# Later places for four steps of the delta heads, and the state's two products side by side

## The chip, the cores and the metric

One core of a Trainium2 chip runs the kernel. The metric is the device time of one execution in microseconds (us), as the median of several runs. Engines are named as in the profile: PE is TensorE (matmuls), DVE VectorE, ACT ScalarE, POOL GpSimd, SP SyncE, which here only issues transfers.

## What is computed

One layer of an encoder, for a prompt of 512 rows and a later chunk of 64 rows that share all weights. The input projection is split into a gated delta rule with 4 heads, a differential attention with 4 heads and a pooling mixer; their outputs are joined, projected back, and a convolutional feed-forward block follows. The change lies in the delta heads:

```python
kk = jnp.einsum('bhncd,bhnsd->bhncs', k, k)
lmat = jnp.where(strict, beta[..., :, None] * decay * kk, 0.0)
uw = lax.linalg.triangular_solve(eye + lmat, rhs, left_side=True, lower=True, unit_diagonal=True)
...
def step(state, xs):
    u_c, w_c, qg_c, qk_c, kt_c, gl_c = xs
    delta = u_c - jnp.einsum('bhcd,bhde->bhce', w_c, state)
    o = jnp.einsum('bhcd,bhde->bhce', qg_c, state) + jnp.einsum('bhcs,bhse->bhce', qk_c, delta)
    state = state * gl_c[..., None, None] + jnp.einsum('bhcd,bhce->bhde', kt_c, delta)
    return state, o
```

The output of each head is then normalised and multiplied by a gate, SiLU(z).

## The kernel before

**The stream.** Most of PE's time goes to gemms: the 576 rows (512 + 64) are the columns of the moving operand, in pieces of 256 and 320, and each weight tile of 128 x 1024 is split into two numbers, `w_hi` (a cast on ACT, L174) and `w_lo` (a subtraction on DVE, L175). A gemm of the input projection is 48 matmuls into a bank `g`. A gemm's end is followed on ACT or DVE by an instruction that empties its bank: L578 for the rows that go through the short convolution, L924 for the attention's rows.

**The planner.** The delta heads and the attention are generators. They `yield` a number, and a clock that adds the nominal time of every matmul issued decides when a generator goes on; its products go into other banks, `m` (four of them), between two matmuls of the stream. `spawn(gen, delay)` starts one. A stream that has to wait for a flag lets the clock jump to the next generator that is due. So the numbers after `yield` fix how many `g` matmuls stand on PE between two steps. PE keeps the order in which the program issues. The other engines' instructions are ordered by a scheduler, and each engine runs its own row in that order.

**The delta heads.** `front(h)` (L609) transposes the keys, the queries and the values of a head (L89 by way of `tokens`), squares them on ACT (L628, L632), scales keys and values (ACT L646) into `kt` and `vs`, and forms five products kk, one for each of five chunks `c` (four of 128 rows, one of 64). The rows to be transposed come from the convolution: DVE taps (L596) and a last product (L601). `levels` (L705) inverts the triangular matrices of two heads in steps of doubling size; its last two steps make `X64` (copied by ACT, L754) and the corner of `XT`. `scan(c)` (L763) goes through the chunks in the order 4, 0, 1, 2, 3, all four heads at once: the state `S` times the key rows gives `R` (DVE), the inverse times `R` gives `e` (copied by ACT, L791), the state times the query rows follows, then `kt` times `e` (the new state, DVE L803) and a product with `e` for the output. Chunk 0 begins without a state. `delta_out` (L825) scales a head's output rows (DVE L833, five instructions), lets 2500 of the clock pass, transposes them, and multiplies them with the gate (L840, L841); `hi` (ACT L844) and `lo` (DVE L845) of the result go to the output projection.

**What waits for what at the end.** When all four heads are through `delta_out`, the attention starts; `value_rows` of its head 0 transposes the values, which sets the flag `values0`. The stream's `attn_proj(3)` waits for that flag before its last projection (L918), since the tile for the values is free only then. The first scores (`ckT` and `kq`) come after that.

Of the kernel before, what the change touches and what calls it, by code (L numbers as in the profile page):

```python
# [11 lines left out]
AF = mybir.ActivationFunctionType  # L12
ALU = mybir.AluOpType
# [46 lines left out]
def hybrid_step(ctx: ExitStack, tc: tile.TileContext, I, O):  # L60
# [30 lines left out]
    def spawn(gen, delay=0):  # L91
        active.append([clock[0] + delay, gen])
# [456 lines left out]
    with ExitStack() as ctx2:  # L549
# [59 lines left out]
        def front(h):  # L609
# [37 lines left out]
            U = dq.tile([P, 5, 2, P], F32, name="U", bufs=4)  # L647
            nc.gpsimd.memset(U[:, 4, :, NS:], 0.0)
            for c in range(5):
                yield 600  # L650
                n = P if c < 4 else NS
                r = slice(starts[c], starts[c] + n)
                kk = bank()[:, :2 * n].rearrange("p (i t) -> p i t", i=2)
                mm(kk, kT[:, starts[c]:starts[c] + P], kq[h][:, :, r])
                Dm = dq.tile([P, P], F32, name="tq", bufs=2)[:, :n]
                nc.vector.scalar_tensor_tensor(Dm, sums[:, c, :n], gsum[:, c, h:h + 1], mneg[:, :n],
                                               op0=ALU.subtract, op1=ALU.add)
                nc.scalar.activation(Dm, Dm, AF.Exp)
                nc.vector.scalar_tensor_tensor(U[:, c, :, :n], kk, w[:, c:c + 1],
                                               Dm.unsqueeze(1).broadcast_to([P, 2, n]), op0=ALU.mult, op1=ALU.mult)  # L660
# [44 lines left out]
        def levels(pair, inv):  # L705
# [44 lines left out]
            for f in pair:  # L750
# [1 line left out]
                for c in range(4):  # L752
                    mm(pa[64:, c * 64:c * 64 + 64], f["K"][:64, c, 64:], f["X64"][:64, c])
                nc.scalar.copy(f["X64"][64:], pa[64:, :256].rearrange("p (c x) -> p c x", c=4))  # L754
            yield 1200
            for f in pair:
                XT = f["T"]
                pa = bank()
# [4 lines left out]
        def scan(c):  # L763
# [14 lines left out]
            for f in heads:  # L778
                f["pa"] = bank()
                if f["S"] is None:  # L780
                    f["R"] = f["vs"][:, c]
                else:
                    mm(f["pa"][:n, 0:P], kq[f["h"]][:, 0, starts[c]:starts[c] + n], f["S"])
                    f["R"] = dq.tile([P, P], F32, name="R", bufs=4)
                    nc.vector.scalar_tensor_tensor(f["R"][:n], f["pa"][:n, 0:P], ngam[:n, c, f["h"]:f["h"] + 1],
                                                   f["vs"][:n, c], op0=ALU.mult, op1=ALU.add)
            yield 1000
            for f in heads:
                mm(f["pa"][:n, P:2 * P], f["T"][:n, c, :n], f["R"][:n])
                f["e"] = dq.tile([P, P], F32, name="e", bufs=4)  # L790
                nc.scalar.copy(f["e"][:n], f["pa"][:n, P:2 * P])  # L791
            if heads[0]["S"] is not None:
                for f in heads:
                    mm(f["pa"][:n, 0:P], kq[f["h"]][:, 1, starts[c]:starts[c] + n], f["S"])
            else:
                yield 420
            for f in heads:
                mm(f["pa"][:, 2 * P:3 * P], f["kt"][:n, c], f["e"][:n])
                Sn = dq.tile([P, P], F32, name="S", bufs=8)
                if f["S"] is None:  # L800
                    nc.vector.tensor_copy(Sn, f["pa"][:, 2 * P:3 * P])
                else:
                    nc.vector.scalar_tensor_tensor(Sn, f["S"], last[:, c, f["h"]:f["h"] + 1],  # L803
                                                   f["pa"][:, 2 * P:3 * P], op0=ALU.mult, op1=ALU.add)
                f["Sn"] = Sn
            for f in heads:
                mm(f["pa"][:n, 3 * P:4 * P], f["Q"][:n, c, :n], f["e"][:n])
            for f in heads:
                oraw = f["o"]
                if f["S"] is None:  # L810
                    nc.scalar.copy(oraw[:n, c], f["pa"][:n, 3 * P:4 * P])
                else:
                    tq = dq.tile([P, P], F32, name="tq", bufs=2)
                    nc.scalar.activation(tq[:n], f["pa"][:n, 0:P], AF.Copy, scale=gam[:n, c, f["h"]:f["h"] + 1])
                    nc.vector.tensor_add(oraw[:n, c], tq[:n], f["pa"][:n, 3 * P:4 * P])
                tq = dq.tile([P, P], F32, name="tq", bufs=2)
                nc.scalar.activation(tq[:n], oraw[:n, c], AF.Square, accum_out=f["sso"][:n, c:c + 1])
                f["S"] = f["Sn"]
                if c == 4:
                    nc.sync.dma_start(O["s_delta"][f["h"]], f["S"])  # L820
                if c == 3:
                    nc.sync.dma_start(O["p_delta"][f["h"]], f["S"])
# [275 lines left out]
        def projections():  # L1098
            nonlocal dq
            for h in range(HEADS):  # L1100
                kq[h], vT[h] = kq_tile(), v_tile()
                first = first_products() if h == 0 else None
                for i, t in enumerate((4 + h, h, 8 + h)):
                    early_rows = h == 0 and i < 2
                    ps = next(first) if early_rows else (yield from gemm(hmix))
                    if not early_rows:
                        yield from after("scaled")
                    conv_rows(t, vT[h] if i == 2 else kq[h][:, i], ps, not early_rows)
                    if h == 0 and i == 1:
                        next(first, None)  # L1110
                        spawn(finish_start(), 3000)
                    if h == 1 and i == 0:
                        yield from after("start")
                        dq = dstack.enter_context(tc.tile_pool(name="delta", bufs=1, reuse_waits="tile"))
                        spawn(front(0), 3500)
                if h:
                    spawn(front(h), 6500)
            spawn(gates(), 0)
# [326 lines left out]
```

## Time and profile before

| what | us |
|---|---|
| median of 3 runs | 851.34 (850.49 to 851.52) |
| the profiled execution | 850.96 |
| its span, first to last instruction | 849.1 |
| outside the span | 1.9 |
| PE busy in the span | 829.5 (98%) |
| DVE, ACT, POOL busy | 536.0, 359.9, 109.5 |

The mean granted clock of TensorE is 0.999. Start times count from the span's beginning. A timeline's row joins instructions of one kind that follow each other, so its duration is that of all of them, and in brackets at its end stands the idle time before it with the instruction that ended it. The delta heads' work lies between about 45 and 275 us.

### The profile page before, as it was taken

The numbers are of one execution on the slowest core, as the hardware profiler recorded it, in microseconds if no ns is written. First come the engines' busy times: TensorE is split into PE (matmuls) and PEld (weight loads), VectorE is DVE, ScalarE is ACT, GpSimd is POOL, SyncE is SP. The second block draws the span as 40 slices with busy tenths as digits, with TensorE's granted clock in tenths as the row PEclk, the third lists the DMA queues.
The fourth block names the chain that finished last, engine by engine and source line by source line (L and its number), as shares of the span: only waits on it lengthen the run. The fifth ranks groups of instructions, "written<-read, shape, count | busy, mean of one in ns | idle before, by whom it ended". The sixth has DMA issues, their size and how long they took to land.

```text
span 849.1 us, 15939 instructions
## 1 busy us (share of the span) xinstructions
PE 829.5 (98%) x6342; PEld 803.9 (95%) x6342; DVE 536.0 (63%) x1203; ACT 359.9 (42%) x798; POOL 109.5 (13%) x166
## 2 busy tenths in 40 slices
PE   9989999999999999999999999999999999999996
PEld 8989999999999877789999999999999999999996
DVE  6798867881348667765767777776776773223423
ACT  7366661163444644543544444444434432222322
POOL 3132211220002000000011121121211210000001
PEclk9999999999999999999999999999999999999999
DMA  6242223242204323326622222222222223323313
GB/s 247 76 125 81 62 72 101 96 117 81 77 32 142 107 80 120 98 77 227 226 75 97 78 75 100 76 78 96 76 84 92 75 74 107 103 87 97 113 58 112
DMA packets 39032, 84.83 MB, mean 100 GB/s; under 512 B 9386, under 2 KB 14526, under 8 KB 38958
## 3 DMA queue, kind: packets, MB, share of 16 engines
q1 hardware_dynamic: 38014, 82.57, 30.1%
q10 hardware_dynamic: 944, 1.25, 0.4%
q8 instruction: 50, 0.82, 0.4%
q14 instruction: 24, 0.20, 0.1%
HBM read 72.98 MB, written 10.82 MB: 99 GB/s over the span
## 4 chain that ended last, share of the span: by engine, by line
PE 89%; DVE 4%; DMA 2%; ACT 2%; issue 1%; SPq 0%; POOLq 0%; POOL 0%; DVEq 0%; ACTq 0%
PE g L85 75%; PE m L85 11%; PE m L89 3%; DMA w_raw<-in_ffn_down_dram 1%; ACT w_hi L174 1%; DVE w_lo L175 1%; DMA x<-in_xT_dram 1%; DVE tmp L890 0%; DVE kq L596 0%; DMA w_raw<-in_w_out_dram 0%; ACT wide L348 0%; DVE oatt L1047 0%; DVE kq L601 0%; DVE p L1016 0%; DVE tmp L578 0%
## 5 line engine op out<-in xcount | busy, mean ns | idle before, releaser
L85 PE MATMUL g<-wide,w_hi 128*128 128x256 f32 x1472 | 265.6, 301 | 0.3
L85 PE MATMUL g<-t,w_hi 128*128 128x256 f32 (+1 forms) x1408 | 242.9, 294 | 0.0
L85 PEld LDWEIGHTS g<-wide,w_hi 128*128 128x128 f32 x1472 | 222.3, 190 | 2.9 <-DVE wide L349 0.6
L85 PEld LDWEIGHTS g<-t,w_hi 128*128 128x128 f32 x1408 | 210.2, 188 | 0.0
L174 ACT CAST w_hi<-w_raw 128x1024 fp32r<-128x1024 f32 (+2 forms) x109 | 110.9, 1017 | 172.8 <-PE g L85 161.8
L85 PE MATMUL g<-wide,w_lo 128*128 128x256 f32 x736 | 160.9, 300 | 0.5 <-DVE w_lo L175 0.5
L175 DVE TENSOR_TENSOR w_lo<-w_raw,w_hi 128x1024 fp32r<-128x1024 f32 (+2 forms) x109 | 128.2, 1176 | 49.9 <-ACT w_hi L174 48.9
L85 PE MATMUL g<-t,w_lo 128*128 128x256 f32 x704 | 150.2, 295 | 0.0
L85 PEld LDWEIGHTS g<-wide,w_lo 128*128 128x128 f32 x736 | 123.7, 190 | 2.5 <-issue 1.1
L85 PEld LDWEIGHTS g<-t,w_lo 128*128 128x128 f32 x704 | 117.4, 188 | 0.1
L1298 DVE SCALAR_TENSOR_TENSOR c<-u,par,c 128x511 f32<-128x511 f32 (+3 forms) x176 | 79.0, 512 | 2.5 <-ACT c L1294 2.5
L1301 POOL COPY fout<-u 128x4 f32<-128x4 f32 x44 | 51.2, 1163 | 223.1 <-DVE u L1292 223.1
L1292 DVE TENSOR_TENSOR u<-g,rstd 128x576 f32<-128x576 f32 x44 | 33.3, 758 | 59.7 <-PE g L85 58.2
L85 PE MATMUL g<-w,w_hi 128*128 128x256 f32 (+1 forms) x280 | 48.4, 295 | 0.0
L85 PEld LDWEIGHTS g<-w,w_hi 128*128 128x128 f32 x280 | 42.0, 188 | 0.0
L1294 ACT ACTIVATE c<-u,par 128x576 f32<-128x576 f32 x44 | 38.4, 873 | 4.6 <-DVE u L1292 1.8
L1318 ACT ACTIVATE s<-c 128x576 f32<-128x576 f32 x22 | 15.1, 688 | 45.8 <-DVE c L1300 45.8
L267 POOL TENSOR_TENSOR osc<-sso,mhalf 128x5 f32<-128x5 f32 x8 | 9.4, 1183 | 182.7 <-DVE sso L1042 77.9
L85 PE MATMUL g<-w,w_lo 128*128 128x256 f32 (+1 forms) x140 | 29.9, 294 | 0.0
L1203 ACT ACTIVATE junk<-m 128x128 f32<-128x128 f32 (+1 forms) x38 | 10.3, 274 | 40.2 <-PE m L89 32.2
L85 PE MATMUL g<-kq,w_hi 128*128 128x256 f32 (+1 forms) x128 | 25.0, 304 | 0.0
L1204 DVE TENSOR_TENSOR t<-m,nf 128x128 f32<-128x128 f32 (+1 forms) x38 | 10.6, 289 | 21.9 <-ACT junk L1203 21.9
(325 smaller groups left out, 1019.8 us busy)
## 6 DMA issues: line engine op xcount, KB each, us to landing
w_raw<-in_ffn_up_dram SPq DMA_DIRECT2D x44, 512.0 KB, 3.2
w_raw<-in_w_in_dram SPq DMA_DIRECT2D x30, 512.0 KB, 3.2
w_raw<-in_ffn_down_dram SPq DMA_DIRECT2D x16, 512.0 KB, 3.6
w_raw<-in_w_out_dram SPq DMA_DIRECT2D x8, 512.0 KB, 3.9
w_raw<-in_ffn_down_dram SPq DMA_DIRECT2D x8, 384.0 KB, 3.2
xr<-in_xT_dram SPq DMA_DIRECT2D x8, 288.0 KB, 3.2
x_d<-xr SPq DMA_DIRECT2D x8, 288.0 KB, 2.1
w<-x_d SPq DMA_DIRECT2D x8, 288.0 KB, 5.2
```

The costliest lines, as they stand in the source:

```text
L85: ordered(nc.tensor.matmul(out, lhsT=lhsT, rhs=rhs, start=start, stop=stop), n / 2.4 if rhs.dtype == F32R else max(54, n / 0.6))
L89: ordered(nc.tensor.transpose(out=out, in_=in_, identity=identity), 107)
L174: nc.scalar.copy(hi[:, :kt], raw)
L175: last_split[0] = nc.vector.tensor_sub(lo[:, :kt], raw, hi[:, :kt].bitcast(F32)).ins
L267: nc.gpsimd.tensor_tensor(out, x, epst[:x.shape[0], :x.shape[1]], op=ALU.pow)
L1203: nc.scalar.activation(junk[:n], src, AF.Square, scale=D ** -0.5, accum_out=op["part"][:n, c, m:m + 1])
L1204: nc.vector.tensor_mul(op["yt"][c][m // 4][:n, (m % 4) * P:(m % 4 + 1) * P], src, op["nf"][:n, m * P:(m + 1) * P])
L1292: nc.vector.tensor_mul(u, ps[:, O0:O1], rstd)
L1294: nc.scalar.activation(c, u, AF.Identity, scale=fw[:, 2, t:t + 1], bias=col("ffn_conv_b", t))
L1298: nc.vector.scalar_tensor_tensor(c[:, a + d:b], u[:, a:b - d], fw[:, j, t:t + 1], c[:, a + d:b], op0=ALU.mult, op1=ALU.add)
L1301: nc.gpsimd.tensor_copy(fout[:, :, :, t], u[:, NP - 64:].rearrange("p (s c) -> p s c", c=64)[:, :, 62:])
L1318: nc.scalar.activation(s, cv[0], AF.Silu)
```

## The change

Four numbers grow: head 0's front starts 7000 instead of 3500 of the clock after its cause, the first kk of every front waits 1700 instead of 600, the last step of `levels` waits 2100 instead of 1200, and in `scan` 900 pass between the copies `e` and the products that use them (before: none, or 420 in chunk 0). And in `scan` both products with the state, of the key rows and of the query rows, are issued at a step's beginning; two regions of the bank change places for that.

```diff
@@ front
             for c in range(5):
-                yield 600
+                yield 600 if c else 1700
@@ levels
-            yield 1200
+            yield 2100
             for f in pair:
                 XT = f["T"]
@@ scan
-                    mm(f["pa"][:n, 0:P], kq[f["h"]][:, 0, starts[c]:starts[c] + n], f["S"])
+                    for i in range(2):
+                        mm(f["pa"][:n, 2 * i * P:2 * i * P + P], kq[f["h"]][:, i, starts[c]:starts[c] + n], f["S"])
...
-            if heads[0]["S"] is not None:
-                for f in heads:
-                    mm(f["pa"][:n, 0:P], kq[f["h"]][:, 1, starts[c]:starts[c] + n], f["S"])
-            else:
-                yield 420
+            yield 900
             for f in heads:
-                mm(f["pa"][:, 2 * P:3 * P], f["kt"][:n, c], f["e"][:n])
+                mm(f["pa"][:, 0:P], f["kt"][:n, c], f["e"][:n])
...
-                    nc.scalar.activation(tq[:n], f["pa"][:n, 0:P], AF.Copy, scale=gam[:n, c, f["h"]:f["h"] + 1])
+                    nc.scalar.activation(tq[:n], f["pa"][:n, 2 * P:3 * P], AF.Copy, scale=gam[:n, c, f["h"]:f["h"] + 1])
@@ projections
-                        spawn(front(0), 3500)
+                        spawn(front(0), 7000)
```

Three places show what this does to the engines' rows. Line numbers after `scan` are smaller by 3 in the changed kernel.

DVE, around head 0's query rows. `kq_150` holds head 0's keys and queries, `kq_534` head 1's; `g_536` and `g_621` are the two gemms of head 1's. Before:

```order
L578 TENSOR_TENSOR tmp_604<-g_536,rstd1_126 128x512
...
L596 SCALAR_TENSOR_TENSOR kq_150<-tmp_304,ah_131,kq_150 128x579 x2
...
L596 SCALAR_TENSOR_TENSOR kq_534<-tmp_604,ah_131,kq_534 128x579
L484 TENSOR_REDUCE lam_138<-lprod_480 128x2
L491 TENSOR_SCALAR qneg_130<-qscale_129 128x5
L439 TENSOR_TENSOR fcor_132<-fcor_132,fcor_t_493 128x44
L601 SCALAR_TENSOR_TENSOR kq_150<-tmp_304,kq_150 128x579
...
L578 TENSOR_TENSOR tmp_713<-g_621,rstd1_126 128x512
```

and now:

```order
L596 SCALAR_TENSOR_TENSOR kq_150<-tmp_304,ah_131,kq_150 128x579
L578 TENSOR_TENSOR tmp_676<-g_621,rstd1_126 128x512
...
L596 SCALAR_TENSOR_TENSOR kq_150<-tmp_304,ah_131,kq_150 128x579
...
L596 SCALAR_TENSOR_TENSOR kq_534<-tmp_604,ah_131,kq_534 128x579
L175 TENSOR_TENSOR w_lo_692<-w_raw_626,w_hi_691 128x1024
L484 TENSOR_REDUCE lam_138<-lprod_480 128x2
L491 TENSOR_SCALAR qneg_130<-qscale_129 128x5
L596 SCALAR_TENSOR_TENSOR kq_534<-tmp_676,ah_131,kq_534 128x579
L439 TENSOR_TENSOR fcor_132<-fcor_132,fcor_t_493 128x44
L601 SCALAR_TENSOR_TENSOR kq_150<-tmp_304,kq_150 128x579
```

The evacuation of `g_621`, a tap on it and a `w_lo` have moved ahead of head 0's L601. On PE the transposes of head 0's keys stand 30 `g` later than before, 12 behind the last matmul of `g_621` (before: 30 into that gemm), and those of the queries 14 behind the keys' in both.

PE, a step of the scan with a state (`R` and `e` as above, `XT` the inverse). Before:

```order
L85 MATMUL m<-R,XT 128x128 x4
L85 MATMUL m<-S,kq 128x128 x4
L85 MATMUL m<-e,kt 128x128 x4
L85 MATMUL m<-e,U 128x128 x4
L85 MATMUL g<-wide,w_hi 128x256
```

and now, where the step begins with both products and 10 `g` stand between them and `R`'s, as before:

```order
L85 MATMUL m<-S,kq 128x128 x8
...
L85 MATMUL m<-R,XT 128x128 x4
L85 MATMUL g<-wide,w_hi 128x256
...
L85 MATMUL g<-wide,w_hi 128x320
L85 MATMUL m<-e,kt 128x128 x4
L85 MATMUL m<-e,U 128x128 x4
```

Eight `g` matmuls now follow `R`'s products. In `levels`, 18 instead of 10 stand between the last two steps.

PE, from head 0's output transposes (`U`) to the value rows (`vT`). Before, 22 `g` stand behind each head's, then two and the value rows, then eight and the scores:

```order
L89 MATMUL m<-cst,U 128x128 x4
L89 MATMUL m<-cst,U 128x64
L85 MATMUL g<-wide,w_hi 128x256
...
L89 MATMUL m<-cst,vT 128x128 x4
L89 MATMUL m<-cst,vT 64x128
```

and now, behind six `g` that follow head 0's:

```order
L89 MATMUL m<-cst,U 128x128 x4
L89 MATMUL m<-cst,U 128x64
L89 MATMUL m<-cst,U 128x128 x4
L89 MATMUL m<-cst,U 128x64
L89 MATMUL m<-cst,U 128x128 x4
L89 MATMUL m<-cst,U 128x64
L89 MATMUL m<-cst,vT 128x128 x4
L89 MATMUL m<-cst,vT 64x128
```

Head 0's transposes stand 62 `g` later than before, the value rows at the same matmul of the stream as before. DVE's row in this stretch is now (`a` are the gates of heads 0 to 3 in this order, `U` the heads' outputs):

```order
L837 SCALAR_TENSOR_TENSOR a_1499<-m_3326,an_h_133,a_1499 128x512
...
L830 TENSOR_SCALAR U_1319<-U_1319,osc_3368 128x128 x4
...
L837 SCALAR_TENSOR_TENSOR a_1611<-m_3354,an_h_133,a_1611 128x512
...
L830 TENSOR_SCALAR U_1603<-U_1603,osc_3389 128x128 x4
...
L175 TENSOR_TENSOR w_lo_3436<-w_raw_3273,w_hi_3435 128x1024
L837 SCALAR_TENSOR_TENSOR a_1710<-m_3375,an_h_133,a_1710 128x512
...
L842 TENSOR_TENSOR kq_3335<-a_1499,kq_3335 128x576
L842 TENSOR_TENSOR kq_3363<-a_1611,kq_3363 128x576
L837 SCALAR_TENSOR_TENSOR a_1771<-m_3396,an_h_133,a_1771 128x512
```

The two heads' scalings stand between gate products whose transposes now follow each other on PE, as they stood between them before with 22 `g` from one to the next.

## Rows read from the trace of the kernel before

**Rows 1.** The page, PE's busy time, share and instructions

```profile
PE 829.5 (98%) x6342; PEld 803.9 (95%) x6342; DVE 536.0 (63%) x1203; ACT 359.9 (42%) x798; POOL 109.5 (13%) x166
```

**Rows 2.** By stretch: length, busy PE, PEld, DVE, ACT, POOL (instructions), granted clock, DMA

```profile
44.00:60.00 16.00, 12.77 (x93) 11.96 (x92) 15.83 (x47) 11.29 (x41) 5.63 (x20) 1.00 0.56 160
60.00:184.00 124.00, 124.00 (x993) 122.75 (x991) 100.69 (x217) 57.76 (x164) 27.04 (x43) 1.00 0.29 88
184.00:193.00 9.00, 8.04 (x75) 7.51 (x74) 5.23 (x12) 5.50 (x14) 1.53 (x6) 1.00 0.27 88
...
225.00:255.00 30.00, 29.31 (x238) 29.05 (x237) 13.36 (x40) 14.03 (x57) 0.56 (x1) 1.00 0.15 50
255.00:277.00 22.00, 22.00 (x160) 20.10 (x160) 17.22 (x55) 8.96 (x19) 4.20 (x4) 1.00 0.48 152
```

**Rows 3.** PE's timeline at head 0's front: start, us, instruction, idle before

```profile
46.98 0.71 PE L89 MATMUL m<-cst,kq 128*128 128x128 f32 x5
...
52.26 1.00 PE L89 MATMUL m<-cst,kq 128*128 128x128 f32 x5 [2.71 <-DVE kq L601]
...
59.00 0.70 PE L85 MATMUL m<-kq 128*128 128x256 f32 x2 [0.51 <-ACT kt L646]
```

**Rows 4.** DVE's timeline at head 0's front

```profile
44.04 1.23 DVE L175 TENSOR_TENSOR w_lo<-w_raw,w_hi 128x1024 fp32r<-128x1024 f32 x1 [0.79 <-ACT w_hi L174]
45.18 0.76 DVE L601 SCALAR_TENSOR_TENSOR kq<-tmp,kq 128x579 f32<-128x579 f32 x1
...
47.26 0.81 DVE L578 TENSOR_TENSOR tmp<-g,rstd 128x512 f32<-128x512 f32 x2
47.99 1.68 DVE L596 SCALAR_TENSOR_TENSOR kq<-tmp,ah,kq 128x579 f32<-128x579 f32 x2
...
50.33 0.81 DVE L596 SCALAR_TENSOR_TENSOR kq<-tmp,ah,kq 128x579 f32<-128x579 f32 x1
51.06 0.28 DVE L484 TENSOR_REDUCE lam<-lprod 128x2 f32<-128x128 f32 x1
```

**Rows 5.** PE's timeline at the second-last step of the levels

```profile
189.19 1.14 PE L85 MATMUL m<-XT,X 64*64 64x64 f32 x16 [0.96 <-ACT X L754]
...
190.63 0.69 PE L85 MATMUL g<-wide,w_hi 128*128 128x256 f32 x4
191.16 0.43 PE L85 MATMUL g<-wide,w_lo 128*128 128x256 f32 x2
```

**Rows 6.** ACT's timeline there

```profile
187.02 1.06 ACT L174 CAST w_hi<-w_raw 128x1024 fp32r<-128x1024 f32 x1
188.10 0.64 ACT L924 COPY vT<-g 128x576 f32<-128x576 f32 x1
```

**Rows 7.** PE's timeline in the scan's chunk 2

```profile
241.63 1.16 PE L85 MATMUL m<-S,kq 128*128 128x128 f32 x8 [0.69 <-ACT e L791]
```

**Rows 8.** ACT's timeline there

```profile
241.31 0.77 ACT L791 COPY e<-m 128x128 f32<-128x128 f32 x4
```

**Rows 9.** PE's timeline at the heads' output: head 0, value rows, scores

```profile
259.40 0.80 PE L89 MATMUL m<-cst,U 128*128 128x128 f32 x5
...
271.83 0.71 PE L89 MATMUL m<-cst,vT 128*128 128x128 f32 x5
...
273.55 1.08 PE L85 MATMUL m<-ckT,kq 64*64 64x512 f32 x4
```

**Rows 10.** DVE's timeline there: a gate product, a scaling, a split, a subtraction

```profile
260.04 0.75 DVE L840 SCALAR_TENSOR_TENSOR a<-m,an_h,a 128x512 f32<-128x512 f32 x1 [0.77 <-PE m L89]
...
260.97 1.05 DVE L833 TENSOR_SCALAR U<-U,osc 128x128 f32<-128x128 f32 x5
...
265.11 1.20 DVE L175 TENSOR_TENSOR w_lo<-w_raw,w_hi 128x1024 fp32r<-128x1024 f32 x1
266.24 0.74 DVE L845 TENSOR_TENSOR kq<-a,kq 128x576 fp32r<-128x576 f32 x1
```

**Rows 11.** A microsecond at the trace's end, columns as in rows 2

```profile
846.00:847.00 1.00, 0.00 (x0) 0.00 (x0) 0.00 (x0) 0.00 (x0) 0.00 (x0) 0.84 0.98 375
```

More of the change, by code (lines that the diff above doesn't have):

```diff
@@ L791, in scan @@
                 nc.scalar.copy(f["e"][:n], f["pa"][:n, P:2 * P])
-            if heads[0]["S"] is not None:
-                for f in heads:
-                    mm(f["pa"][:n, 0:P], kq[f["h"]][:, 1, starts[c]:starts[c] + n], f["S"])
-            else:
-                yield 420
+            yield 900
             for f in heads:
-                mm(f["pa"][:, 2 * P:3 * P], f["kt"][:n, c], f["e"][:n])
+                mm(f["pa"][:, 0:P], f["kt"][:n, c], f["e"][:n])
                 Sn = dq.tile([P, P], F32, name="S", bufs=8)
                 if f["S"] is None:
-                    nc.vector.tensor_copy(Sn, f["pa"][:, 2 * P:3 * P])
+                    nc.vector.tensor_copy(Sn, f["pa"][:, 0:P])
                 else:
                     nc.vector.scalar_tensor_tensor(Sn, f["S"], last[:, c, f["h"]:f["h"] + 1],
-                                                   f["pa"][:, 2 * P:3 * P], op0=ALU.mult, op1=ALU.add)
+                                                   f["pa"][:, 0:P], op0=ALU.mult, op1=ALU.add)
                 f["Sn"] = Sn
```

## The prediction

> **What bounds the kernel now.** I read the share of the span by engine first, then busy time by stretch, and then, for each stretch in which TensorE (PE) sits idle, its timeline with the engine it waits for. PE is busy 98% of the span [rows 1], so the time falls only where PE now stands still, and rises wherever it is made to. The stretches are the reader's main view [rows 2]: from 44 to 60 us PE is busy 12.77 of 16 us, from 60 to 184 all of it, from 184 to 193 8.04 of 9, from 225 to 255 29.31 of 30, and from 255 to 277 all of it. So in everything that the change touches 3.23 + 0.96 + 0.69 = 4.88 us of idle can be won, and the last stretch, the delta heads' output, has nothing to win and only something to lose. The filling of PE's time is matmuls `g` at a steady pace: four from 190.63 to 191.16, 0.133 us each [rows 5].
>
> **Front of head 0: later, and still late.** The transposes of the keys run at 46.98; those of the queries start at 52.26 after 2.71 us idle, waiting for VectorE (DVE) line 601; a product kk stands 0.51 us at 59.00 for ScalarE (ACT) line 646 [rows 3]. A wait costs some 0.1 us more than its idle, as the work before it drains uncovered; by PE's pace the queries were wanted at 49.4, so I take 2.87 and 0.78, 3.65 us together. In the changed order this front stands 30 `g` later, 30 x 0.133 = 4.0 us: queries wanted at 53.4. But DVE's queue has moved as well. The scheduler now lets head 1's query rows go first: ahead of head 0's line 601 stand the evacuation of `g_621` (line 578), one more tap and a `w_lo`, and the evacuation must wait for the end of that gemm, which falls at about 49.4 (head 0's transposes no longer interrupt it). Counted from 49.5 by start-to-start distances [rows 4]: evacuation 0.73 (47.26 to 47.99), head 0's tap 0.8 (half of 1.68), the small ones 0.7, a tap 0.73, `w_lo` 1.14 (44.04 to 45.18), small ones 0.3, a tap 0.75, small 0.1, line 601 0.76: it ends at 55.5. The stall is 55.6 - 53.4 = 2.2 us instead of 2.87. The kk that waits for ACT's fourth scaled key block finds it about 0.4 us late (before 0.78), since a cast of 1.05 us at the gemm's end now precedes the scaling; I allow 0.25 for one more such short wait. 3.65 becomes 2.85: **0.8 us gained**, between 0 (the wait moves whole) and 3.65 (all gone). The first kk of every front waits 1700 instead of 600; in fronts 2 and 3, between 60 and 184 us, PE loses nothing now, so that is worth nothing there; its cover is the same pace of `g`.
>
> **Levels: the last step.** At 189.19 PE had waited 0.96 us for ACT's copy X [rows 5]. ACT had cast a weight (1.06) and emptied a gemm's bank (0.64) right before [rows 6]; the pair comes at every gemm's end, each 48 `g`. The order puts 18 `g` instead of 10 between the two steps: 8 x 0.133 = 1.07 us more cover for about 1.0 us of wait. **1.0 us gained** (0.6 to 1.0); the second pair of heads showed no wait and has none to give.
>
> **Scan.** In step c=2 PE waits 0.69 us at 241.63 for the copies e [rows 7], which ACT makes from 241.31 behind the same pair [rows 8]. The products with the state's query rows stood behind R's, and at 241.63 they waited in front of kt's; now they stand in front, 8 `g` follow R's products, and kt·e comes after those. 8 `g` are 1.07 us, more than the wait: **0.8 us gained** (0.4 to 1.2, with the small waits of the other steps). In c=1 the step now begins 4 `g` ahead of a gemm's end and its R 6 behind: ACT is free after 1.7 us, four copies take 0.8, and kt is wanted 2.7 us after the end, so 0.2 us is left. All products remain; a step enters the gemm stream three times rather than twice, which no row prices. One more matmul of 128 columns per step, 0.1 us, bounds it from above, nothing from below; I take **0.1 us lost** over the four steps (0 to 0.4).
>
> **Output of the heads: the new loss.** Head 0's transposes now stand 62 `g` later, and the main stream's end doesn't move: it stops for "values0", which head 0's value rows set only after the four heads' output. Before, 22 `g` (2.9 us) stood between one head's transposes and the next's. Now 6 stand behind head 0, and then heads 1, 2, 3 and the value rows come one behind another with no `g` at all. What then sets the time is DVE, whose order is: head 0's gate products, head 2's scaling, head 1's gate, head 3's scaling, a `w_lo`, head 2's gate (which frees the banks for the value rows), two `lo` subtractions, head 3's gate (which frees those for the scores). From the end of head 0's transposes, start to start, by [rows 10]: gate 0.9 (260.04 to 260.97, less a small one between), scaling 1.0, gate 0.9, scaling 1.0, `w_lo` 1.13 (265.11 to 266.24), gate 0.9: the value rows can start at 5.8. Two `lo` 1.4 (0.74 printed for each) and a gate 0.9: the scores at 8.1. PE's own work there is 6 `g` 0.8, three sets of transposes 3 x 0.73 (0.80 printed [rows 9]) and, from the value rows to the scores, 1.72 (271.83 to 273.55): 4.7. So **3.4 us lost**, in pieces of at most 1.5. Below, 2 if the scheduler's gate products run shorter or half overlapped; above, 5 if the two waits on ACT inside this chain (its cast and its `hi` copies) come last.
>
> The DVE queue does this because nothing overtakes in it: head 0's gate product at 260.04 starts 0.64 us after its transposes do [rows 9, 10], and the scaling that was queued behind it, at 260.97, has been ready for long; the changed order queues head 3's scaling behind head 1's gate product in the same way. [...]
>
> **Sum.** -0.8 - 1.0 - 0.8 + 0.1 + 3.4 = +0.9 us, on the profiled execution's 850.96: 851.9. The profiled execution stands 0.4 us below the median of the runs, 851.34; against that it is **852.2 us**. A measurement of this kernel can tell about 0.2%, 1.7 us, from no change.
>
> **Rivals.**
> *All waits go, 849.3 us.* If head 0's line 601 is early enough at the new place, the front gives 3.65 instead of 0.8: 852.2 - 2.9 = 849.3, just over 0.2% faster; with the tail at its lower end of 2 us it is 847.9. For it: 4 us of later place against 2.9 of wait. Against it: DVE is busy 15.83 of the 16 us from 44 to 60 [rows 2], and three large instructions have come in front. It decides where line 601 ends: before 53.4.
> *The waits move with the work, 854.4 us.* The front's 3.65 stay, because DVE and not the place sets them, and the copies e in c=1, with 0.2 us to spare, come late: 852.2 + 0.8 + 0.4, and with 1 us more in the tail, whose chain leaves PE nothing to do, 854.4, slower. One mechanism: DVE and ACT queues run at their own pace and PE catches up with them. It decides where line 601 ends after 56.3, and the scores start over 9 us behind head 0's transposes.
> [...]
> *Nothing changes hands, 851.3 us.* Gains and the tail cancel, or the tail's loss is taken up by later slack: it lies within 0.2% and beside my forecast.
>
> **How the numbers follow.** Forecast with its own spread (850.3 to 853.6) 0.5; all waits go, or the tail cheap, 0.22; the waits move 0.23; the clock 0.05. Of the forecast's 0.5 some 0.08 lies above 853.04 (slower), little below 849.64. Faster 0.23, same 0.42, slower 0.35. The range takes in the first rival near its lower price and the second: 848.2 to 855.0.
>
> **What would show it.** In the changed profile: the wait for line 601 near 2.2 us at about 53.5; no wait for X near 189 and none for e over 0.3 us; PE idle about 3.4 us in pieces after head 0's transposes near 265, with the gate products (line 837) and line 842 as the releasers; the clock 1.00 through them. The forecast is wrong if PE is busy through that stretch, or if the front's wait is gone.

## The result: 8 us slower, outside the forecast's range

The changed kernel takes 859.78 us (median of 4 runs, 857.64 to 862.85) where the kernel before takes 851.43 beside it (4 runs, 850.49 to 852.50): a ratio of 1.0098, interval 1.0077 to 1.0118. The forecast was 852.2, with 855.0 as the upper end. The profiled execution took 857.64, with a span of 855.9 (before 849.1) and a mean granted clock of 0.995 (before 0.999).

By stretch, as in [rows 2], with the columns as there (length, busy PE, PEld, DVE, ACT, POOL, granted clock, DMA), the changed kernel:

```profile
40.00:70.00 30.00, 26.86 (x200) 26.18 (x199) 27.40 (x69) 17.18 (x51) 9.19 (x27) 1.00 0.38 116
...
170.00:184.00 14.00, 11.85 (x116) 11.47 (x115) 12.00 (x24) 4.77 (x9) 1.62 (x4) 1.00 0.48 138
184.00:200.00 16.00, 14.30 (x150) 13.49 (x149) 7.75 (x19) 8.91 (x26) 1.52 (x6) 0.89 0.20 56
...
225.00:262.00 37.00, 37.00 (x295) 36.41 (x294) 16.21 (x44) 16.35 (x65) 0.00 (x0) 1.00 0.18 59
262.00:292.00 30.00, 27.67 (x195) 24.21 (x194) 22.91 (x76) 14.21 (x36) 5.12 (x4) 1.00 0.42 137
```

Length less PE's busy time is PE's idle time. The front still loses 3.14 us (before 3.23). The levels, 170 to 200 us, lose 3.85 (before 0.96), and there the granted clock falls as well. The scan loses nothing (before 0.69). The heads' output loses 2.33 (before nothing). PE's idle time in the whole span is 4.5 us more than before, and PE is busy 831.8 instead of 829.5 us, which I put down to the lower clock (the stretch from 188 to 192 us alone, at 0.50 and 0.67, makes 1.7 of it); 4.5 + 2.3 are the span's 6.8. The forecast's sum for the idle time was +0.9 us.

What PE waits for (line waited for: us in total, times, longest):

```profile
PE m L85 <- DMA Xc<-inv: 2.1, 2, 1.2
PE m L89 <- DVE kq L601: 2.1, 1, 2.1
...
PE m L85 <- ACT XT L722: 1.7, 1, 1.7
...
PE m L85 <- ACT kt L646: 1.0, 1, 1.0
```

Two of these rows, `Xc` and `XT` L722, stand for 3.8 us in a place where the prediction had no cost at all.

**Where the levels' wait comes from.** The inversion of the small blocks (31 rounds of L687 and L689 on DVE) ends with a store of `inv` on SP, and the levels load that as `Xc`. DVE's timeline of the kernel before, at the inversion's end:

```profile
168.79 0.22 DVE L689 TENSOR_TENSOR kq<-kq 80x60 f32<-80x60 f32 x1
169.04 0.19 DVE L687 TENSOR_TENSOR kq<-a,kq 80x31 f32<-80x31 f32 x1
169.26 0.19 DVE L689 TENSOR_TENSOR kq<-kq 80x31 f32<-80x31 f32 x1
...
170.71 0.74 DVE L922 TENSOR_TENSOR kq<-g,rstd 128x576 f32<-128x576 f32 x1
```

and of the changed kernel:

```profile
169.14 0.22 DVE L689 TENSOR_TENSOR kq<-kq 80x60 f32<-80x60 f32 x1
170.27 0.76 DVE L919 TENSOR_TENSOR kq<-g,rstd 128x576 f32<-128x576 f32 x1 [0.91 <-PE g L85]
170.94 0.18 DVE L687 TENSOR_TENSOR kq<-a,kq 80x31 f32<-80x31 f32 x1
171.08 1.23 DVE L175 TENSOR_TENSOR w_lo<-w_raw,w_hi 128x1024 fp32r<-128x1024 f32 x1
172.22 0.18 DVE L689 TENSOR_TENSOR kq<-kq 80x31 f32<-80x31 f32 x1
```

Before, the last round (80x31) ends at 169.45, 1.26 us before the evacuation of a gemm's bank starts (L922). Now the last head's front ends 1.1 us of the clock later, the first round starts 1.55 us later (135.40 instead of 133.85), and the last round stands behind the evacuation (L919) in DVE's order: the evacuation and the weight split, 1.9 us together, run ahead of 0.36 us of work. The last row ends 2.95 us later. Little of that is lateness. The round before the last (80x60) ends at 169.36 instead of 169.01, 0.35 us later; then DVE stands idle for 0.91 us until the gemm ends. The last round, whose inputs are the rounds before it, stands right behind the evacuation. So 2.6 of the 2.95 us come from the order that the scheduler made, not from DVE having too much to do. Of all 14 traces, the four whose last head's front has 1700 (this kernel and the runs with the kk number alone, with closer rounds and with the store on ACT's queue) show this order and this idle time of 0.90 or 0.91; the ten others have the last round ahead of the evacuation. Why the scheduler turns the order round is not shown. Then the store. SP's timeline before, and after:

```profile
166.64 0.37 SPq L167 DMA_DIRECT2D w_raw<-in_w_in_dram  x1
169.48 0.33 SPq L691 DMA_DIRECT2D inv<-kq  x1
...
172.14 1.64 SPq L718 DMA_DIRECT2D Xc<-inv  x2
```

```profile
171.05 0.34 SPq L1063 DMA_DIRECT2D out_k_dram<-kq  x1
172.33 0.33 SPq L167 DMA_DIRECT2D w_raw<-in_w_in_dram  x1
172.71 1.00 SPq L691 DMA_DIRECT2D inv<-kq  x1
178.16 0.95 SPq L718 DMA_DIRECT2D Xc<-inv  x2
```

The loads of `Xc` wait for the store: 2.66 us after its issue before, 5.45 us now, when a weight of 512 KB (issued 0.4 us ahead of it) and an output of 288 KB (1.7 us ahead) are under way beside it; which of the two slows it isn't shown. So 3.2 us on DVE and 2.8 us in the DMA engines make 6.0 us on `Xc`, against 1.3 us by which the planner moved the levels. PE's timeline shows where it lands:

```profile
180.23 0.65 PE L85 MATMUL m<-Xc,U 32*32 32x32 f32 x18 [0.93 <-DMA Xc<-inv]
182.09 0.65 PE L85 MATMUL m<-Xc,U 32*32 32x32 f32 x18 [1.22 <-DMA Xc<-inv]
...
187.50 0.31 PE L85 MATMUL m<-Y,XT 32*32 32x32 f32 x5 [1.70 <-ACT XT L722]
```

The first two waits, 2.15 us, are for the loads. The third is for ACT's copies of the second head's transposed `Xc` (L722), and there the order has changed as well. ACT:

```profile
183.09 1.34 ACT L722 COPY XT<-XTc 32x160 f32<-32x160 f32 x4
185.84 0.27 ACT L707 ACTIVATE X<-m 32x128 f32<-32x128 f32 x1 [1.41 <-PE m L85]
...
186.70 1.33 ACT L722 COPY XT<-XTc 32x160 f32<-32x160 f32 x4
```

DVE had transposed the second head's block by 184.80, but its copies stand behind three instructions (L707) that need PE's products of the first head, and ACT idles 1.41 us in front of those. In the kernel before the second head's copies stand ahead of them (180.66, then L707 from 182.03). The same four traces have the new order on ACT, the ten others the old one.

**And the clock.** Stretches of 2 us in the changed kernel, columns as above:

```profile
178.00:180.00 2.00, 1.29 (x10) 1.06 (x8) 1.88 (x3) 0.03 (x1) 0.00 (x0) 1.00 0.33 53
180.00:182.00 2.00, 0.65 (x18) 0.54 (x18) 1.51 (x5) 0.28 (x1) 1.05 (x2) 1.00 0.90 226
...
186.00:188.00 2.00, 0.50 (x18) 0.53 (x18) 0.98 (x4) 1.92 (x7) 0.00 (x0) 0.98 0.25 40
188.00:190.00 2.00, 2.00 (x18) 1.90 (x16) 1.83 (x4) 1.22 (x6) 0.00 (x0) 0.50 0.03 8
190.00:192.00 2.00, 2.00 (x12) 2.00 (x12) 1.00 (x2) 1.43 (x4) 0.00 (x0) 0.67 0.51 124
```

Behind several thin stretches, the last with PE busy for 0.50 of 2 us, the granted clock is 0.50 from 188 to 190 us, PE's first full stretch in a while, and 0.67 in the next 2 us.

### The profile page after: what moved, and what is told of

Read it like the earlier page. It is cut to its first block, busy times and chain, and to the rows that moved or that the text cites. A ratio compares the mean times of both kernels' runs of the same rounds, so it can differ in the third digit from the quotient of the medians.

```text
span 855.9 us, 15946 instructions
## 1 busy us (share of the span) xinstructions
PE 831.8 (97%) x6342; PEld 806.4 (94%) x6342; DVE 535.6 (63%) x1203; ACT 358.5 (42%) x798; POOL 108.1 (13%) x166
## 4 chain that ended last, share of the span: by engine, by line
PE 89%; DVE 4%; DMA 4%; ACT 2%; issue 1%; SPq 0%; POOL 0%; POOLq 0%; DVEq 0%; ACTq 0%
PE g L85 75%; PE m L85 12%; PE m L89 2%; DMA w_raw<-in_ffn_down_dram 1%; DVE w_lo L175 1%; DMA x<-in_xT_dram 1%; DMA inv<-kq 1%; DMA XT<-gsum_d 1%; DMA Xc<-inv 0%; DMA w_raw<-in_w_out_dram 0%; ACT wide L348 0%; ACT w_hi L174 0%; DVE oatt L1044 0%; DVE kq L601 0%; DVE a L837 0%
```

## The experiments

Every run lists the mean granted clock of its span, and in all these kernels the slower runs are mostly those with the lower clock. I fitted one common slope over all runs of all kernels (each with a level of its own): 0.59 us per 0.001 of mean clock. The last column is a kernel's mean time brought to a clock of 0.999 with that slope, an estimate of what it would take without falls of the clock; the difference of the median to it is put down to the clock. It is worked out, not measured: a kernel's runs scatter about it by 0.3 to 0.8 us, and the five runs of the kernel before that had a clock of 0.999 took 850.3 to 851.2 us, above the 849.9 of the column. So differences between its rows say more than the rows themselves, and those under a microsecond say little.

| kernel | runs | median us | median clock | at clock 0.999 |
|---|---|---|---|---|
| before (all comparisons) | 74 | 851.86 | 0.996 | 849.9 |
| after | 4 | 859.78 | 0.991 | 855.4 |
| after, kk at 600 | 10 | 856.78 | 0.994 | 853.8 |
| after, inversion's rounds closer | 5 | 860.61 | 0.991 | 855.2 |
| after, last head's kk at 600 | 4 | 856.28 | 0.992 | 852.1 |
| after, store from ACT's queue | 5 | 858.51 | 0.992 | 854.2 |
| before, kk at 1700 | 7 | 856.54 | 0.991 | 851.4 |
| before, front and levels | 6 | 857.27 | 0.994 | 854.0 |
| before, scan | 10 | 853.20 | 0.9955 | 851.0 |
| before, later output only | 4 | 855.76 | 0.9915 | 851.4 |
| before, with extra matmuls | 5 | 855.37 | 0.994 | 852.2 |
| before, front and levels in place | 10 | 851.35 | 0.995 | 849.2 |
| the same, all rows tied | 12 | 854.54 | 0.9935 | 851.3 |
| the same, taps tied | 12 | 850.59 | 0.996 | 848.5 |

**Four runs to find the part that costs.** The first undoes the kk number in the changed kernel.

```diff
-                yield 600 if c else 1700
+                yield 600
```

> The changed kernel with the first kk of each front at 600 again; front of head 0, levels and scan stay changed. Theory A (the kk number delays the 31-round inversion on DVE by 1.2 us, its last rows then fall behind a weight split, and its store runs beside a weight load): the store of the inverse is issued near 169.5 us again and not 172.7, PE has no wait for Xc, the granted clock stays 1.00 through the levels, and the time drops by 4 to 6 us to 854 to 855.5, with the 2.3 us of idle at the heads' output left. Theory B (the later places of front, levels and scan, whatever the inversion does, cost the time): 858 or more, and the waits for Xc stay.

856.78 us, ratio 1.0047 (1.0031 to 1.0062). The wait for `Xc` is gone, and from 170 to 200 us PE is busy all of it at full clock. SP's timeline:

```profile
169.43 0.37 SPq L167 DMA_DIRECT2D w_raw<-in_w_in_dram  x1
172.27 0.33 SPq L691 DMA_DIRECT2D inv<-kq  x1
...
174.93 1.51 SPq L718 DMA_DIRECT2D Xc<-inv  x2
```

The whole stream is 2.8 us late here by then, so the store is not at 169.5; but the last round stands ahead of the bank's evacuation again, the store is issued with the last weight load 2.8 us old, and it lands in 2.6 us. The gain was 3 us and not 4 to 6, because the number had been worth something in the front. PE there, and its clock:

```profile
64.15 0.70 PE L85 MATMUL m<-kq 128*128 128x256 f32 x2 [2.36 <-ACT kt L646]
```

```profile
62.00:64.00 2.00, 0.00 (x0) 0.00 (x0) 2.00 (x6) 1.81 (x8) 1.42 (x4) 1.00 0.59 156
...
66.00:68.00 2.00, 2.00 (x8) 1.82 (x8) 1.55 (x3) 0.17 (x1) 0.00 (x0) 0.50 0.39 152
```

A second long wait follows 8 us behind that for L601, and behind it the clock is 0.50 from 66 to 68 us.

The second run is the number alone, in the kernel before.

```diff
-                yield 600
+                yield 600 if c else 1700
```

> The kernel before with only the first kk of each front at 1700. Theory A: nearly all of the loss in the levels comes with this one number: 4 to 6 us slower than before, 855.5 to 857.5, with the store near 172.7, waits for Xc and a clock under 1.00 near 188 us. Theory B: within 1.5 us of before (851 to 853), since the later kk alone moves little.

856.54 us, ratio 1.0055 (1.0020 to 1.0090): as theory A had it. The store is issued at 173.10, 0.4 us behind a weight load, `Xc` at 178.62, and the waits of 2.1 (Xc) and 1.7 us (XT) are those of the changed kernel. Its clock falls more (0.75 from 184 to 200 us). Its runs go from 850.27 to 861.71; the fastest, without a profile, has a clock of 0.999, which doesn't fit a wait of that size in the levels. DVE's order is set when the program is built, so how this execution came out is open. This profile also shows the front's gap, the same 2.7 us as in [rows 3], with another outcome for the clock:

```profile
50.00:52.00 2.00, 0.00 (x0) 0.00 (x0) 2.00 (x11) 1.07 (x6) 0.00 (x0) 1.00 1.04 301
52.00:54.00 2.00, 1.69 (x8) 1.69 (x9) 2.00 (x11) 1.46 (x13) 0.66 (x2) 0.50 1.18 302
```

The third run shifts the inversion's rounds in the changed kernel.

```diff
-                yield 840
+                yield 800
```

> The changed kernel with the inversion's rounds 800 instead of 840 of the clock apart, so that its 31 rounds end 1.24 earlier. Theory A: it is the inversion's end that decides, so this wins back what the kk number costs, without touching it: the store at 169 to 170 us, no waits for Xc, 854 to 855.5. Theory B, or a rival by which the kk products themselves cost it: 858 or more.

860.61 us: a miss. The store stays behind the split (173.97) and all waits stay. The planner's distance only fixes which rows stand in front of which on DVE, and the last round still stood behind the evacuation, with DVE idle for 0.90 us in front of it. So ending the rounds earlier by the planner's clock did not change the order, and the order is what costs.

The fourth has front and levels only.

```diff
-            yield 1200
+            yield 2100
@@
-                        spawn(front(0), 3500)
+                        spawn(front(0), 7000)
```

> The kernel before with front 0 at 7000 and the levels' last step at 2100 only. The prediction's terms: front -0.8, levels -1.0, and some of the heads' output loss (the planner ends 1.8 us later, so only the last head's transposes and the value rows close up): 850 to 852. Theory B: the later levels bring the loss, 855 or more.

857.27 us, ratio 1.0052 (1.0033 to 1.0070): above the 850 to 852 of the prediction's terms. It is in theory B's range, but not for its reason, since the levels lose nothing (170 to 200 us busy throughout). The front has waits of 2.1 and 2.6 us and a clock of 0.50, as the first run. The rest of the loss is new, in the scan, which this kernel does not change: 900 per pair of heads move its steps against the gemms' ends. PE, and DVE at the third of the waits:

```profile
230.98 0.49 PE L85 MATMUL m<-e,U 128*128 128x128 f32 x2 [0.79 <-DVE S L801]
245.60 0.49 PE L85 MATMUL m<-S,kq 128*128 128x128 f32 x2 [1.63 <-DVE U L815]
```

```profile
243.35 1.22 DVE L175 TENSOR_TENSOR w_lo<-w_raw,w_hi 128x1024 fp32r<-128x1024 f32 x1 [1.00 <-ACT w_hi L174]
244.49 0.86 DVE L785 SCALAR_TENSOR_TENSOR R<-m,ngam,vs 128x128 f32<-128x128 f32 x3
```

Again a weight split stands in front of a step's small instructions.

**The inversion's start by itself.** Only the last head's front goes back to 600.

```diff
-                yield 600 if c else 1700
+                yield 600 if c or h == HEADS - 1 else 1700
```

> The changed kernel with the first kk of the last head's front back at 600; heads 0 to 2 keep 1700. The last head's front is what the inversion starts from. If the levels' loss comes from the inversion ending behind a gemm's weight split, this run has no wait for Xc and full clock from 170 to 200 us, while head 0's front keeps its one wait of about 1 us at the kk: 854 to 855.5 us, faster than the changed kernel and than the run with 600 everywhere (856.8). If the levels' waits come with the later front of heads 0 to 2, they stay and the time is 858 or more.

856.28 us, ratio 1.0056 (1.0041 to 1.0071), 3.5 us under the changed kernel and 3.3 less at equal clock. PE is busy all of 170 to 200 us at full clock, the store is issued at 170.34 and lands in 2.6 us. The place is right; the time is 0.8 us over the range I gave, as the clock still falls elsewhere (0.94 from 262 to 292 us). That the kk number causes the levels' loss is shown, and that it does so in the last head's front: in the kernel before the number alone brings the loss, and in the changed kernel it is gone when that one front has 600 again. It is not the whole miss. Without the levels' loss this kernel is still 4.6 us slower than the kernel before beside it (851.67), above the forecast's upper end of 855.0; by the column at equal clock 2.2 of that are waits, the rest is the clock.

**The output by itself.**

```diff
             yield from until(lambda: "gates" in done)
+            yield 7020
             for h in range(HEADS):
                 yield from delta_out(fs[h])
```

> The kernel before with nothing but 7020 more of the clock ahead of the heads' output, so that heads 1 to 3 and the value rows close up as in the changed kernel. The prediction's term: PE idle 3.4 us in that stretch (2 to 5), the time of before plus as much, 854 to 856. The changed kernel's own trace shows 2.3 us there: 853.5 to 855. A rival by which the clock falls in the stretch: 857 or more, with a granted clock under 1.00 between 270 and 290 us.

855.76 us, ratio 1.0057 (1.0039 to 1.0075): in the range of the prediction's term, but not by its 2 to 5 us of idle time. The waits in the stretch come to 1.05 us, one wait ahead of the value rows, and most of the rest goes with the lower clock of its runs (median 0.9915):

```profile
274.34 0.76 PE L89 MATMUL m<-cst,vT 128*128 128x128 f32 x5 [1.05 <-DVE a L840]
```

Here the scaling of all heads was done by 265, long before the chain began. In the changed kernel two scalings of about 1 us lie inside it, and two `lo` subtractions instead of one stand ahead of the last gate product; it loses 2.33. The difference of 1.3 us is roughly what both together are worth: 0.9 up to the value rows, where DVE's row differs in the scalings (on PE eight `g` stand behind head 0's transposes here, six there), and 0.4 at the scores. The clock didn't fall in this stretch (1.00 from 262 to 292 us).

**The scan by itself.** All of the scan's part of the change, in the kernel before; cut to its core:

```diff
-                    mm(f["pa"][:n, 0:P], kq[f["h"]][:, 0, starts[c]:starts[c] + n], f["S"])
+                    for i in range(2):
+                        mm(f["pa"][:n, 2 * i * P:2 * i * P + P], kq[f["h"]][:, i, starts[c]:starts[c] + n], f["S"])
...
+            yield 900
```

> The kernel before with only the scan's part of the change (both products with the state first, 900 of the clock before kt times e). The prediction's terms: 0.8 us won in the scan, no wait for e over 0.3 us, and most of the heads' output loss, as the chain is 4 us later: +1 to +3 us, 852.5 to 855. If the products' new order itself brings waits, a wait for DVE's R or S over 0.5 us shows in the scan and it is 856 or more.

853.20 us, ratio 1.0016 (1.0002 to 1.0029): in the range of the terms, but not by them. The wait for `e` is gone, as forecast. In its place PE waits 0.81 us for S (L800), in chunk 0, and 0.36 later in the scan:

```profile
221.50 0.94 PE L85 MATMUL m<-e,U 64*64 64x128 f32 x6 [0.81 <-DVE S L800]
245.18 0.71 PE L85 MATMUL m<-S,kq 128*128 128x128 f32 x4 [0.36 <-DVE U L812]
```

That is 1.17 us where the kernel before had 0.69, so the scan loses about 0.5 us instead of winning 0.8, and the output loses 0.07 instead of most of 3.4.

**Is it the clock that scatters the kernel before?** Nine matmuls whose result is overwritten fill the wait of [rows 3].

```diff
+            pq_bank = bank()
+            if h == 0:
+                keep_busy(pq_bank[:, :P], kT[:, :P], 9)
-            pq = tokens(qT, bank(), 1)
+            pq = tokens(qT, pq_bank, 1)
```

> The kernel before with nine extra matmuls of 128 columns (1.8 us, their result is overwritten) on PE just ahead of head 0's query transposes, in the 2.7 us in which PE waits there. Theory C (this idle time lowers the clock in some executions, and that is the scatter of the kernel before): the runs stay within 1 us of 850.5, median 850.0 to 851.0, mean clock 0.997 or more in all. Rival (the scatter comes from somewhere else): as before, median near 852 with runs up to 855.

855.37 us: a miss. The nine matmuls fit, and in the profiled execution everything runs as before up to 360 us; then the clock falls once between 360 and 380 us (0.96 and 0.87 in two stretches of 10 us, 0.98 as the mean from 360 to 440), and 3.5 us are lost there, about 1.0 of them in longer waits. So this gap isn't the only place, and filling it does not steady the kernel. That its runs are slower than before's in the attention is not explained.

**The store's queue.**

```diff
-            nc.sync.dma_start(inv_d, xf)
+            nc.scalar.dma_start(inv_d, xf)
```

> The changed kernel with one edit: the store of the inverse is issued from ACT's queue instead of SP's, where it stands 0.4 us behind a weight load. If that load ahead of it makes the store land 5.5 instead of 2.7 us after its issue, it now lands within 3.5 us, the loads of Xc are issued by 176.5 us (before 178.2), the waits for Xc (2.1 us) go or fall under 0.7, and the time falls by 2 to 4 us to 856 to 858. If the delay is the store's own or the late last row of the inversion on DVE alone suffices, the Xc loads stay near 178 us and the time near 860.

858.51 us (856.10 to 862.83), 1.2 less than the changed kernel at equal clock. The store is issued at 172.34, the loads of `Xc` at 177.35: still 5.0 us. That fits neither expectation: the loads do not come by 176.5, and the time is between 858 and 860. So the queue's order is not what makes the store slow; the weight load (0.1 us ahead) and the output of 288 KB (1.4 us ahead) are under way beside it as before. The waits for `Xc` fall to 0.5 us as its loads come 0.8 earlier. The 1.7 us for `XT` stay, since they come from ACT's order and not from the loads.

**A version that keeps what works.** It takes the kernel before, gives head 0's front more room, and makes up for the levels' 900 inside the levels, so that the inversion, the scan and the output stand where they stood.

```diff
-            yield 1530
+            yield 1530 if h else 4500
@@
-                yield 600
+                yield 600 if c or h else 1700
@@ levels
-            yield 6000
+            yield 6000 if pair[0]["h"] == 0 else 4200
@@
-            yield 1200
+            yield 2100
```

> The kernel before with three of the change's ideas, placed so that nothing behind them moves: 1700 ahead of the first kk in head 0's front only, head 0's query transposes 4500 instead of 1530 behind its keys', and 2100 ahead of the levels' last step, made up for by 4200 instead of 6000 ahead of the second pair's first step. The inversion, the scan and the heads' output stand as before. By the runs so far: the kk's wait of 0.5 and the levels' of 0.96 go; the query transposes' wait stays near 2 us, since the scheduler puts head 1's rows on DVE ahead of head 0's line 601 again once there seems to be time. Idle 1.5 to 2 us less than before, 849 to 851 where before has about 851.7. Rival: the later query transposes do help as the clock sees it, and line 601 is early enough: 847.5 to 849.

851.35 us, ratio 0.9998 (0.9988 to 1.0009): no difference to measure. The levels' wait is gone, PE waits 1.36 us for L601 and 0.42 for L646; 0.7 us are won at equal clock, which is within the scatter. As expected, line 601 moved behind head 1's rows on DVE with the room it was given.

Tying head 1's rows behind it (`first_rows` holds head 0's line 601):

```diff
+                    with ExitStack() as pinned:
+                        if h == 1 and i < 2:
+                            pinned.enter_context(tc.issue_after(first_rows[0]))
-                    conv_rows(t, vT[h] if i == 2 else kq[h][:, i], ps, not early_rows)
+                        conv_rows(t, vT[h] if i == 2 else kq[h][:, i], ps, not early_rows)
```

> The same, and head 1's first two sets of convolution rows are tied to come after head 0's line 601 on DVE. Then line 601 ends near 52.5 us, where the query transposes are now wanted: PE idle under 1 us between 44 and 70 us (before 3.23), none in the levels, clock full there: 3 us less than before, 847.5 to 849.5, with less scatter than before. Rival: tying the rows makes head 1's gemm banks come free late, and PE waits for them instead (a wait of g for line 578 or of head 1's key transposes): no gain, 851 or more.

854.54 us, ratio 1.0032 (1.0021 to 1.0043): the rival. The profile's list of waits begins with

```profile
PE g L85 <- DVE tmp L581: 3.8, 1, 3.8
```

The evacuation of a gemm's bank had been tied as well, and the gemms waited for it.

Only the taps tied (weights 1 and 5 are head 1's queries and keys):

```diff
             for j in (2, 1, 0):
+              with ExitStack() as pinned:
+                if t in (1, 5):
+                    pinned.enter_context(tc.issue_after(first_rows[0]))
                 tap = nc.vector.scalar_tensor_tensor(c, u[:, j:j + n], ahw[:, j, t:t + 1], c, op0=ALU.mult, op1=ALU.add)
```

> As the run that kept the heads' chain in place (query transposes 4500 behind the keys', 1700 for head 0's first kk, levels made up for), but with only head 1's taps tied to come after head 0's line 601, not the evacuation of its gemm banks. Then no gemm waits for line 578 (3.8 us with everything tied), line 601 ends 1.5 us earlier than without the tie, and the query transposes wait under 0.5 us: idle 40 to 70 us under 1 us, 849 to 850.5 where before has 851.7, a small gain. Rival: the wait moves to head 1's rows or the time is set by the clock elsewhere: 851 or more.

850.59 us, ratio 0.9975 (0.9958 to 0.9992), faster than both kernels, by 1.3 us against the kernel before and 0.1 over the range I gave. The query transposes wait 0.63 us; a wait of 1.53 for ACT's scaled values (L654 there) has come at a kk, which I did not expect, so that 2.2 us are idle from 40 to 70 us where I had said under 1.

```profile
53.34 0.77 PE L89 MATMUL m<-cst,kq 128*128 128x128 f32 x5 [0.63 <-DVE kq L607]
...
62.21 0.70 PE L85 MATMUL m<-kq 128*128 128x256 f32 x2 [1.53 <-ACT vs L654]
```

## Why the prediction was wrong, step by step

**The step that failed first** is the half sentence on fronts 2 and 3: that the first kk's 1700 "is worth nothing there; its cover is the same pace of `g`". PE's cover was right, but I followed the moved front only on PE. The last front's blocks go through a store to the inversion on DVE, and its store goes to the levels. With the number, the inversion's last round stands behind a gemm's evacuation and weight split on DVE, and the second head's copies stand behind the first head's on ACT. [rows 2] couldn't show it, since PE was busy there all the time. I had DVE's changed order, in which the last row stands behind the split, and did not look at it there. In the levels 1.0 us was to be won. The wait for X did go, as forecast; new waits of 3.85 us came, so that the levels lose 2.9 more idle than before and, in the profiled execution, about 1.7 to the clock (16 us at a mean of 0.89).

**The clock** had a chance of 0.05, with the output as its place. It fell in the levels (0.89 from 184 to 200 us), and in other runs in the front (0.94 from 40 to 70), the output (0.94 from 262 to 292) and the attention (0.95 to 0.98, as means over 68 or 80 us). I took [rows 3] and one level of 1.00 in [rows 2] as a sign that such a gap does no harm; the same gap, in the run with only the kk number, left 0.50. At the medians it makes some 2.4 of the 8 us, by the estimate of the table (859.78 - 855.4 = 4.4 after, 851.86 - 849.9 = 2.0 before); with four runs after, that is a rough share. It is the second reason for the miss: the run without the levels' loss is still outside the range.

**Front:** 2.10 us of wait for L601 stood against 2.2 forecast, and the reason, DVE's queue, was the one given. The kk waited 1.04 us instead of 0.4. Sum 3.14 idle: 0.1 won instead of 0.8. The term for the kk was too small, and the sum started too high: 3.65 us for two waits whose idle time is 2.71 and 0.51, so 0.43 added where the text says some 0.1 for each (by [rows 5], four `g` print 0.69 us and the next starts 0.53 behind their start, so the last one runs on for 0.16).

**Scan:** 0.69 won, 0.8 forecast, and the closeness is luck. The wait for `e` went as forecast in every run that has the scan's part. But in the kernel before, the scan's part by itself loses 0.5, and in the changed kernel without the levels' loss (the runs with 600 in every front, and in the last one) PE waits 0.9 us for S and 0.2 more. Only where the levels come late did the scan's steps escape those waits. The term for entering the stream a third time, 0.1 us (0 to 0.4), was too small. I had looked for a collision on ACT, in c=1, and not on DVE.

**Output:** 2.33 us lost against 3.4. The mechanism is the forecast's, with DVE's chain as the releaser of each wait. PE:

```profile
271.79 0.80 PE L89 MATMUL m<-cst,U 128*128 128x128 f32 x5
...
275.53 1.03 PE L89 MATMUL m<-cst,U 128*128 128x128 f32 x5 [0.51 <-DVE U L830]
278.02 0.77 PE L89 MATMUL m<-cst,vT 128*128 128x128 f32 x5 [1.46 <-DVE a L837]
280.20 1.27 PE L85 MATMUL m<-ckT,kq 64*64 64x512 f32 x4 [0.36 <-DVE a L837]
```

From DVE's first gate product (272.43) to the scores are 7.8 us, where I had counted 8.1; PE's own part was mis-sized, 4.7 counted, 7.8 - 2.3 = 5.5 seen, since each set of transposes prints 0.80 or more where I took 0.73, and value rows and matmuls up to the scores took 1.8 (278.02 to 280.20 less 0.36) where I took 1.72; the rest I did not trace. That the scalings in the chain, with one subtraction, cost about 1.3 us is seen against the run with the later output alone. The row that the prediction gave for DVE's order, in which nothing overtakes, does not show it: the scaling at 260.97 had not "been ready for long", as its factor came from POOL only at about 260.4 (259.22 and 1.17 us), after the gate product's start at 260.04. DVE's 0.91 us of idle time in front of L919, with the last round ready behind it, does. On ACT the 1.41 us of idle time in front of L707 agrees, as the second head's copies stood behind it with their block transposed by 184.80. I applied that order to two places and not to the third.

**The rivals.** "The waits move with the work" was nearest: its place (L601 later than 56.3) was wrong, its idea, that DVE's and ACT's queues and not the planner's places set the time, was right, in the levels.

## What to carry to other kernels

A step that is moved by a microsecond must be followed to its consumers on every engine and queue, also where the engine that bounds the kernel is busy throughout: look in the changed order of each for an instruction that others wait for and that has come to stand behind a periodic burst (here each gemm's evacuation and weight split of 1.9 us) or behind work that waits for another engine. Spare time in the old trace is no safe measure: here a last round that was 0.35 us later ended 2.95 us later. Where a scheduler orders the other engines, room given to a consumer can be used up by moving its producer back (here 1.36 us of the wait for line 601 stayed); tie the producer's place, and only that. And a kernel that waits on its bounding engine can lose clock in one execution and not in the next (with the kk number alone, the runs' mean clock went from 0.983 to 0.999): judge it by many runs and by the granted clock of each.

## What the runs showed of the hardware

The front's gap of 2.7 us on PE left the granted clock at 1.00 in two traces (the kernel before, and with the later output only) and went with a lower one in two others (a mean of 0.94 from 40 to 70 us both with the kk number alone, where it was 0.50 from 52 to 54, and with the scan's part alone), so a trace with a full clock doesn't prove a gap harmless. Most of a kernel's scatter goes with its mean clock here: 0.59 us per 0.001, with the kernel before between 850.3 us at 0.999 and 857.6 at 0.987. In four traces DVE stood idle for 0.90 or 0.91 us in front of an instruction that was not ready, with a ready one behind it in its row. And a store of 320 KB that landed 2.6 to 2.7 us after its issue where no transfer had been issued in the 2.8 us ahead of it took 5.0 to 5.5 us, up to the issue of the loads that wait for it, where a load of 512 KB and a store of 288 KB had been issued in the 1.7 us ahead of it, from the same queue as these or from another.
